# Delta-rule stage of a fp32 hybrid layer: base blocks and decay masks turned and filled on chip, low weight parts by accumulating transfers

## The chip, the cores and the metric

The kernel runs on one core of one Trainium2 chip. The metric is the device time of one execution in microseconds. A core has TensorE (PE, whose weight loads are listed apart as PEld), VectorE (DVE), ScalarE (ACT), GpSimd (POOL) and SyncE (SP). Here nearly all transfers are issued from SP's queue.

## The reference

One layer over 512 latent tokens of width 1024, with 256 context tokens: half-step SwiGLU FFN, then two mixers side by side (neighbourhood attention; bidirectional gated DeltaNet) merged by sigmoid gates, then a second half-step FFN. The change lies in the gated delta rule, which works on chunks of 64 tokens:

```python
    decay = jnp.exp(jnp.where(lower, g[..., :, None] - g[..., None, :], -jnp.inf))
    m = jnp.where(strict, jnp.einsum('...ik,...jk->...ij', k_beta, k) * decay, 0.0)
    rhs = jnp.concatenate([v * beta[..., None], k_beta * jnp.exp(g)[..., None]], axis=-1)
    uw = lax.linalg.triangular_solve(jnp.eye(GDN_CHUNK) + m, rhs, left_side=True, lower=True, unit_diagonal=True)
    def step(s, xc):
        v_new = xc[0] - jnp.einsum('...ck,...kv->...cv', xc[1], s)
        s_next = s * xc[3][..., None, None] + jnp.einsum('...ck,...cv->...kv', xc[2], v_new)
        return s_next, (jnp.einsum('...ck,...kv->...cv', xc[4], s) + jnp.einsum('...cj,...jv->...cv', xc[5], v_new))
```

There are four heads and two directions. The kernel takes chunks of 128 tokens, six in each direction (two of context, four of latent), and inverts the 128 x 128 triangular matrices explicitly.

## The kernel before

Matrix products in fp32 are made of three: a weight tile is split into a high part `wh` (a rounded copy, ACT, line 137) and a low part `wl` (weight minus high part, DVE, line 139), an activation likewise into `uxh` and `uxl`, and hi·hi, hi·lo and lo·hi are accumulated (`mm3k`, lines 192 to 194). Class `Stream` loads the next weight block (`wr`, 512 KB, SP) and splits it, one block ahead, into two buffers each of `wh` and `wl`.

Projections of the mixers whose results are needed only later (queries, keys and values of the attention, `qa`, `ka`, `va`, and the gates `ga`, `gb`) are "fills": each is 24 matmuls of 128x512 into one accumulator `pm`, copied out by ACT (`spill`) and stored to DRAM. They are cut into FS = 4 quarters of six matmuls. In the delta-rule stage, `turn(kind, i)` adds a rate from the table `RATE` (g: Grams, l: ahead of the first inversion, i: inversions, s: scan) to a running debt and emits a quarter for each whole unit, marked to be issued behind the last delta-rule matmul. So PE has fill work to do while the other engines finish what the next small delta-rule matmul needs. 24 fills stand in this stage. The text is given to a scheduler that orders each engine's instructions by a modelled timeline; `issue_after` marks add edges to it.

The delta rule itself goes by steps s = 0 to 5 (one chunk in each direction) and head pairs p = 0, 1; two steps make a batch, bi = 0, 1, 2. The stage's parts are:

- `gram(p, s)`: the row of cumulated decay logs `gcd` is loaded over all partitions into `Dt` (256 KB; for s below 3 into parts of `oacc`). DVE subtracts the column and adds the triangular mask, four times 128x128 (line 1122), ACT takes the exponential over 512 columns (line 1123). DVE multiplies product, beta and decay into `Bt` (line 1128), stored to DRAM as `bd`, and for s of 2 and over product and decay into `At` (line 1134). Products come from PE (`pq`) or, for s of 4 and 5, from copies in DRAM (`kq`).
- `base_inverse`, once a batch: 64 diagonal 32x32 blocks are inverted together, row by row. The blocks come back from `bd` by six kinds of loads with short pieces into `L` and `Ltr`; ACT turns `Ltr` (line 1153), POOL fills the diagonal (line 1155) and the start `Xt`. Then 31 rows follow, each a product and a reduction on DVE (lines 1159, 1160). `Xt` is stored to DRAM as `rd`.
- `inverse(bi, st)`, twice a batch: the inverted blocks are read from `rd` into `T0` and `T1` (SP, eight transfers a batch), DVE transposes the other halves (lines 1182, 1183), ACT and POOL copy them into `T6` and `Tt` (line 1194). Then the blocks grow 32 to 64 to 128 by PE products `pi`, with DVE copies `Y` (lines 1202, 1229) and negated results written into `T6` (DVE, line 1218) and `Tt` (ACT, lines 1219, 1237) between them.
- `scan_step(p, s)`: the recurrence on the states `S`, PE products `pc` with DVE and ACT work between them.
- `gdn_out`: norm and gate, then the stage is over.

The program's order is: Grams and base blocks of batch 0, Grams of batch 1, inversions of batch 0 with the rows of batch 1 between them, scans of batch 0 with the Grams of batch 2, and so on, so that the rows of one batch run beside the inversions and scans of the one before. POOL's queue before holds only memsets, the `Tt` copies and a few small operations in this stage.

Of the kernel before, what the change touches and what calls it, by code (L numbers as in the profile page):

```python
# [58 lines left out]
def body(ctx, tc, I, out, dbg=None):  # L59
# [96 lines left out]
    class Stream:  # L156

        def __init__(self, wp, srcs, bufs, ahead):  # L160
# [946 lines left out]
    def decay_place(s, p):  # L1107

        if s == 2 or s < 2 and p == 1:
            a = 2 * (s == 2)  # L1110
            return oaccs[p if s == 2 else s][:, a:a + 2].rearrange("p a b c -> p (a b) c")
        return tl(gb_, [P, 4, P], "Dt", 2)[:]

    def gram(p, s, bd, g):
# [3 lines left out]
        nc.sync.dma_start(Dt[:], bass.AP(gcd.tensor, gcd.offset + (4 * s + 2 * p) * P, [[0, P], [24 * P, 2], [1, 2 * P]]))  # L1118
        for m, (d, c, i) in enumerate(mats):
            msk = cst[:, (C_MF if d == 0 else C_MB):][:, 0:P]  # L1120
            with tc.issue_after(marks["At" if s > 3 else "Bt"]) if s > 1 else nullcontext():
                V.scalar_tensor_tensor(Dt[:, m], Dt[:, m], gcum[:, d, s, 2 * p + i:2 * p + i + 1], msk, op0=ALU.subtract, op1=ALU.add)
        S.activation(Dt[:], Dt[:], AF.Exp)
        Bt, At = tl(gq, [P, 4, P], "Bt", NBT), None
        for n, t in enumerate(products(p, s)):
            if n == 0:
                for m, (d, c, i) in enumerate(mats):
                    b = V.scalar_tensor_tensor(Bt[:, m], t[m] if s == 1 else t[:, m], beta[:, d, s, 2 * p + i:2 * p + i + 1], Dt[:, m], op0=ALU.mult, op1=ALU.mult)
# [11 lines left out]
    def base_inverse(bd, rd):  # L1140


        L = tl(gb_, [P, 32, 32], "L")
# [9 lines left out]
        S.copy(L[0:64].rearrange("p r c -> p c r"), tr[:])

        G.memset(L[:].rearrange("p r c -> p (r c)")[:, 0:1024:33], -1.0)
        for i in range(1, 32):
# [3 lines left out]
            V.tensor_reduce(Xt[:, 0:c, i], t[:, 0:c, 0:i + 1], AX, ALU.add, negate=True)  # L1160
# [12 lines left out]
    def inverse(bi, st, rd, Bts):  # L1173


        T0 = tl(gq, [P, 8, 32], "T0", 2)
        T1 = tl(gq, [P, 8, 32], "T1", 2)
        for dst, d in ((T1, 0), (T0, 1)):
            for q in range(2):
                nc.sync.dma_start(dst[q:P:2, 4 * d:4 * d + 4], bass.AP(rd.tensor, rd.offset + (2 * d + q) * 16384 + st * 2048, [[32, 64], [2 * 2048, 4], [1, 32]]))  # L1180
# [737 lines left out]
```

## Time and profile before

| what | value |
|---|---|
| median of 3 runs | 1499.81 us (1499.24 to 1501.12) |
| profiled execution | 1495.44 us |
| its span | 1493.7 us |
| mean granted PE clock | 0.993 |
| PE busy, whole span | 1434.0 us (96%) |
| DVE / ACT / POOL busy, whole span | 1144.7 / 661.9 / 212.4 us |
| delta-rule stage | 733.2 to 966.4 us of the span |

Busy times are of the profiled execution; the engine idle least, PE, is the one on which most of the chain of waits lies (71% of it), with transfers at 10% and DVE at 9%. Weight loads (PEld) overlap the matmuls. A wait line "PE pi L1049 <- DVE Y L1229" reads: a matmul of line 1049 into `pi` waited for DVE's write of `Y` on line 1229.

### The profile page before, as it was taken

Reading aid. Unit: us, or ns where it says so; the run is one execution under the profiler, and the core shown is the slowest. Engines: PE = TensorE matmul, PEld = TensorE weight load, DVE = VectorE, ACT = ScalarE, POOL = GpSimd, SP = SyncE. Lnnn points to the kernel's source line nnn. Section 1 sums busy time; section 2 is a strip of 40 time slices with the busy share of each in tenths; the row PEclk is TensorE's granted clock in tenths of the full one; section 3 lists DMA queues with packets and bytes.
Section 4 is the critical chain, followed back from the end, with each engine's and each line's share of the span. In section 5 each row is a group of like instructions: output and inputs, shape, how many; then the busy total and the mean of one; then the engine's idle time right before and its main releaser. Section 6 shows DMA issues by size and latency. Waiting matters only on the chain.

```text
span 1493.7 us, 23926 instructions
## 1 busy us (share of the span) xinstructions
PE 1434.0 (96%) x9117; PEld 1258.3 (84%) x9117; DVE 1144.7 (77%) x1975; ACT 661.9 (44%) x1090; POOL 212.4 (14%) x262
## 2 busy tenths in 40 slices
PE   6999999999999999999998899999999999999997
PEld 4778989999998777888886778877778999998886
DVE  8787869999987565768787886666668799886627
ACT  5433524434333286545544434376526454444310
POOL 1000000000000121223301002243321022220001
PEclk9999999999999999999999999999999999999999
DMA  9676665454559554222577524274344143234732
GB/s 372 211 257 225 222 238 187 137 174 166 170 198 404 181 178 129 84 92 88 159 222 203 167 68 125 92 276 131 100 169 149 64 129 113 85 114 134 263 98 84
DMA packets 109236, 248.56 MB, mean 166 GB/s; under 512 B 29049, under 2 KB 44481, under 8 KB 109121
## 3 DMA queue, kind: packets, MB, share of 16 engines
q1 hardware_dynamic: 104480, 229.40, 46.6%
q0 software_dynamic: 3056, 12.33, 2.2%
q10 hardware_dynamic: 1586, 5.32, 0.9%
q8 instruction: 71, 1.16, 0.3%
q14 instruction: 43, 0.35, 0.1%
HBM read 215.50 MB, written 31.50 MB: 165 GB/s over the span
## 4 chain that ended last, share of the span: by engine, by line
PE 71%; DMA 10%; DVE 9%; ACT 4%; issue 3%; POOL 1%; SPq 1%; DVEq 0%; ACTq 0%; POOLq 0%
PE ps L211 15%; PE pm L192 5%; PE pm L193 5%; PE pm L194 5%; PE ps L533 4%; PE ps L535 4%; PE ps L534 4%; PE ps L1692 3%; PE ps L1694 3%; PE ps L1693 3%; PE ps L193 3%; PE ps L192 3%; PE ps L194 3%; PE pc L1049 3%; DMA wr<-in_up_dram 2%
## 5 line engine op out<-in xcount | busy, mean ns | idle before, releaser
L139 DVE TENSOR_TENSOR wl<-wr,wh 128x1024 fp32r<-128x1024 f32 (+1 forms) x184 | 226.0, 1233 | 112.9 <-ACT wh L137 111.3
L137 ACT CAST wh<-wr 128x1024 fp32r<-128x1024 f32 (+1 forms) x184 | 185.6, 1013 | 278.5 <-PE pm L193 72.7
L192 PE MATMUL pm<-uxh,wh 128*128 128x512 f32 x320 | 131.6, 411 | 0.0
L194 PE MATMUL pm<-uxh,wl 128*128 128x512 f32 x320 | 126.3, 395 | 0.8 <-DVE wl L139 0.8
L193 PE MATMUL pm<-uxl,wh 128*128 128x512 f32 x320 | 126.5, 395 | 0.0
L211 PE MATMUL ps<-wh,hx 128*128 128x512 f32 x352 | 96.1, 391 | 0.1
L211 PEld LDWEIGHTS ps<-wh,hx 128*128 128x128 f32 x352 | 65.9, 188 | 14.5 <-ACT wh L137 0.5
L280 DVE SCALAR_TENSOR_TENSOR adap<-wr,crow 128x1024 f32<-128x1024 f32 x61 | 74.3, 1218 | 2.4 <-DMA wr<-in_w_adaT_dram 1.7
L192 PE MATMUL ps<-uh,wh 128*128 128x256 f32 (+1 forms) x208 | 69.2, 334 | 3.8 <-ACT wh L137 3.8
L194 PEld LDWEIGHTS pm<-uxh,wl 128*128 128x128 f32 x320 | 60.6, 190 | 13.8 <-DVE wl L139 0.9
L192 PEld LDWEIGHTS pm<-uxh,wh 128*128 128x128 f32 x320 | 60.8, 190 | 11.1 <-ACT spill L796 0.2
L193 PEld LDWEIGHTS pm<-uxl,wh 128*128 128x128 f32 x320 | 60.9, 190 | 10.3
L114 POOL TENSOR_TENSOR rs<-ve,mhalf 128x1 f32<-128x1 f32 (+2 forms) x46 | 49.0, 1066 | 140.6 <-DVE ve L110 138.2
L193 PE MATMUL ps<-ul,wh 128*128 128x256 f32 (+1 forms) x208 | 67.9, 327 | 0.0
L194 PE MATMUL ps<-uh,wl 128*128 128x256 f32 (+1 forms) x208 | 67.0, 328 | 0.0
L193 PE MATMUL ps<-uxl,wh 128*128 128x256 f32 (+1 forms) x192 | 60.5, 318 | 2.2 <-DVE uxl L139 2.2
L192 PE MATMUL ps<-uxh,wh 128*128 128x256 f32 (+1 forms) x192 | 59.8, 318 | 1.6 <-ACT uxh L137 1.4
L194 PE MATMUL ps<-uxh,wl 128*128 128x256 f32 (+1 forms) x192 | 60.1, 316 | 0.0
L137 ACT CAST wh<-ra 128x1024 fp32r<-128x1024 f32 x31 | 32.6, 1052 | 59.7 <-PE ps L534 20.2
L533 PE MATMUL ps<-ur,wh 128*128 128x384 f32 x168 | 56.5, 336 | 0.0
L534 PE MATMUL ps<-ur,wh 128*128 128x384 f32 x168 | 56.4, 336 | 0.0
L533 PE MATMUL ps<-uh,wh 128*128 128x384 f32 x168 | 56.4, 336 | 0.0
(502 smaller groups left out, 4252.0 us busy)
## 6 DMA issues: line engine op xcount, KB each, us to landing
wr<-in_w_adaT_dram SPq DMA_DIRECT2D x64, 512.0 KB, 4.7
wr<-in_up_dram SPq DMA_DIRECT2D x56, 512.0 KB, 3.6
wr<-in_win_dram SPq DMA_DIRECT2D x52, 512.0 KB, 3.6
wr<-in_dn_dram SPq DMA_DIRECT2D x51, 512.0 KB, 4.1
ra<-in_up_dram SPq DMA_DIRECT2D x24, 512.0 KB, 4.3
rb<-in_up_dram SPq DMA_DIRECT2D x18, 512.0 KB, 4.0
ra<-in_w_adaT_dram SPq DMA_DIRECT2D x16, 512.0 KB, 5.0
wr<-in_w_o_dram SPq DMA_DIRECT2D x8, 512.0 KB, 4.4
```

What stands on the lines that cost most here:

```text
L114: G.tensor_tensor(rs[:], ve[:], mhalf[:, 0:n], ALU.pow)
L137: S.copy(hi, src)
L139: marks["lo"] = V.tensor_tensor(lo, src, hi.bitcast(F32), ALU.subtract).ins
L192: T.matmul(ps, a, uh[:, k, :], start=(k == 0), stop=False)
L193: T.matmul(ps, a, ul[:, k, :], start=False, stop=False)
L194: marks["mm"] = T.matmul(ps, b, uh[:, k, :], start=False, stop=(k == nk - 1)).ins
L211: T.matmul(banks[t][d][:, c0:c1], a[:, sl], b[:, d * 512 + c0:d * 512 + c1], start=first and j == 0, stop=last and j == 2)
L280: V.scalar_tensor_tensor(pr[:], raw[:], 1.0, crow, op0=ALU.mult, op1=ALU.mult, accum_out=col[:, c:c + 1])
L533: T.matmul(ps[:], a, mh, start=k == 0, stop=False)
L534: T.matmul(ps[:], a, ml, start=False, stop=False)
L535: T.matmul(ps[:], b, mh, start=False, stop=k == 3)
L1049: last[0] = T.matmul(*a, **k).ins
```

## The change

Five things are changed together, all in the delta-rule stage.

1. **Low parts.** For the 24 fills of the stage (`ws.dma`), DVE's subtraction goes. ACT writes the negated high part into `wl`, in two halves, and POOL issues for each half a transfer of 256 KB from `wr` onto `wl` that adds to what is there. Every fill now does its 16 products with the high part first and its eight with the low part last (also where the low parts are made as before).
2. **Base blocks.** The way through DRAM (`bd`) goes. ACT copies the diagonal blocks from `Bt` into a tile `W` (four copies a Gram, 48 in all); DVE transposes part of `W` in 32x32 blocks, then all of it into `L`, and sets the diagonal. The start of `Xt` is loaded from a constant, `xt0`.
3. **Inverted rows.** The way through DRAM (`rd`) goes. DVE transposes `Xt` into `Z`, ACT copies halves into `T0` and `T1` (two copies for each of the two inversions), DVE transposes the other halves.
4. **Masks.** For s of 2 and over SP loads the mask (`msk`, a constant of 256 KB) into the decay tile and POOL issues a transfer that adds the row; ACT takes the exponential per matrix, 128x128, with the negated column as its bias. For s below 2 it stays as before. `issue_after` marks put the row for s = 5 behind the `Tt` copies and the exponentials behind the W copies of the batch before or, for s = 5, behind the last `Tt` write. For s = 3 the decay tile is now a buffer `r`.
5. **Rates.** g (2, 3.0, 0.7) to (2, 2.4, 0.6); l 7.2 to 2; i (1.5, 0, 0) to (1.2, 0.2, 0.7); s (0.7, 0.9, 0.5) to (0.6, 0.8, 0.9). The number of fills in the stage stays 24.

The core of the diff:

```diff
+    def split_dma(src, hi, lo):
+        S.copy(hi, src)
+        n = src.shape[-1] // 2
+        for h in (slice(0, n), slice(n, 2 * n)):
+            S.activation(lo[:, h], hi[:, h].bitcast(F32), AF.Copy, scale=-1.0)
+            G.dma_start(lo[:, h], src[:, h], accum_op=ALU.add)
...
-        for k in range(KT):
-            if k and k % (KT // parts) == 0:
+        prods = [(w[0], u, k) for k in range(KT) for u in (uxh, uxl)] + [(w[1], uxh, k) for k in range(KT)]
+        for n, (a, u, k) in enumerate(prods):
+            if n and n % (3 * KT // parts) == 0:
                 yield
-            mm3k(px[:], w[0], w[1], uxh, uxl, k)
+            marks["mm"] = T.matmul(px[:], a[:, k * P:k * P + P], u[:, k, :], start=n == 0, stop=n == 3 * KT - 1).ins
...
-    RATE = {"g": (2, 3.0, 0.7), "l": (7.2,), "i": (1.5, 0, 0), "s": (0.7, 0.9, 0.5)}
+    RATE = {"g": (2, 2.4, 0.6), "l": (2,), "i": (1.2, 0.2, 0.7), "s": (0.6, 0.8, 0.9)}
...
+    def blocks(W, Bt, p, st):
+        m0 = 4 * st + p
+        for b in range(4):
+            r = slice(32 * b, 32 * b + 32)
+            marks["W"] = S.copy(W[r, 8:24].rearrange("p (d m) c -> p d m c", d=2)[:, :, m0:m0 + 3:2], Bt[r, :, r].rearrange("p (d i) c -> p d i c", d=2)).ins
...
+        if s > 1:
+            nc.sync.dma_start(Dt[:], I["msk"])
+            with tc.issue_after(marks["Tt"]) if s > 4 else nullcontext():
+                G.dma_start(Dt[:], row, accum_op=ALU.add)
+        else:
+            nc.sync.dma_start(Dt[:], row)
...
+            if s > 1:
+                with tc.issue_after(marks["Ti" if s > 4 else "Wg"]):
+                    S.activation(Dt[:, m], Dt[:, m], AF.Exp, bias=ngc[:, d, s, 2 * p + i:2 * p + i + 1])
...
-                nc.sync.dma_start(bass.AP(bd.tensor, bd.offset + g * MSTR, [[P, P], [4 * MSTR, 4], [1, P]]), Bt[:])
+                blocks(W, Bt, p, s % 2)
...
-        for q in range(4):
-            dst = tr[32 * q:32 * q + 32] if q < 2 else L[32 * q:32 * q + 32]
-            nc.sync.dma_start(dst, bass.AP(bd.tensor, bd.offset + (q // 2) * 8 * MSTR, [[st, 32], [P, 32], [1, 32]]))
-        S.copy(L[0:64].rearrange("p r c -> p c r"), tr[:])
-        G.memset(L[:].rearrange("p r c -> p (r c)")[:, 0:1024:33], -1.0)
+        with tc.issue_after(marks["Z"]) if "Z" in marks else nullcontext():
+            V.transpose(W[:, 0:8].rearrange("p m c -> p (m c)"), W[:, 16:24].rearrange("p m c -> p (m c)"))
+        V.transpose(L[:].rearrange("p r c -> p (r c)"), W[:, 0:16].rearrange("p m c -> p c m")[:, :, None].to_broadcast([P, 32, 2, 16]))
+        V.memset(L[:].rearrange("p r c -> p (r c)")[:, 0:1024:33], -1.0)
...
-        nc.sync.dma_start(bass.AP(rd.tensor, rd.offset, [[512, P], [1, 512]]), Xt[:].rearrange("p c k -> p (c k)"))
+        Z = tl(gb_, [P, 16, 32], "bt")
+        marks["Z"] = V.transpose(Z[:].rearrange("p c k -> p (c k)"), Xt[:].rearrange("p c k -> p (c k)")).ins
+        z = Z[:].rearrange("p c (q m) -> p m (c q)", q=2)
+        for st in range(2):
+            S.copy(T0[:, 0:4], z[:, 4 * st + 8:4 * st + 12])
+            S.copy(T1[:, 4:8], z[:, 4 * st:4 * st + 4])
+            V.transpose(fl(T1, 0), fl(T0, 0))
+            V.transpose(fl(T0, 4), fl(T1, 4))
```

How the instructions stand is shown at three places. The first is PE ahead of the first inversion of batch 0; `pm` is the accumulator of a fill, `pi` of the inversion, `Bt` the product blocks. Before:

```order
L194 MATMUL pm_7609<-uxh_4690,wl_7572 128x512
L192 MATMUL pm_7609<-uxh_4690,wh_7571 128x512
L193 MATMUL pm_7609<-uxl_4691,wh_7571 128x512
L194 MATMUL pm_7609<-uxh_4690,wl_7572 128x512
L192 MATMUL pm_7609<-uxh_4690,wh_7571 128x512
L193 MATMUL pm_7609<-uxl_4691,wh_7571 128x512
L194 MATMUL pm_7609<-uxh_4690,wl_7572 128x512
L1049 MATMUL pi_7644<-T_1408_7628,Bt_7012 32x32 x4
L1049 MATMUL pi_7644<-T_1408_7628,Bt_7042 32x32 x4
L1049 MATMUL pi_7644<-T_1408_7628,Bt_7012 32x32 x4
L1049 MATMUL pi_7644<-T_1408_7628,Bt_7042 32x32 x4
```

and with the change:

```order
L803 MATMUL pm_7559<-uxl_4691,wh_7481 128x512
L803 MATMUL pm_7559<-uxh_4690,wl_7482 128x512 x8
L803 MATMUL pm_7596<-uxh_4690,wh_7552 128x512
L803 MATMUL pm_7596<-uxl_4691,wh_7552 128x512
L803 MATMUL pm_7596<-uxh_4690,wh_7552 128x512
L803 MATMUL pm_7596<-uxl_4691,wh_7552 128x512
L803 MATMUL pm_7596<-uxh_4690,wh_7552 128x512
L803 MATMUL pm_7596<-uxl_4691,wh_7552 128x512
L1064 MATMUL pi_7611<-T_1341_7253,Bt_7015 32x32 x4
L1064 MATMUL pi_7611<-T_1341_7253,Bt_7051 32x32 x4
L1064 MATMUL pi_7611<-T_1341_7253,Bt_7015 32x32 x4
L1064 MATMUL pi_7611<-T_1341_7253,Bt_7051 32x32 x4
```

Before, nine fills and three quarters of the tenth stand between the start of the stage and the first `pi`; now seven and a quarter, and the eight products with `wl` stand together at a fill's end.

The second is DVE at the last rows of batch 0's base blocks. Before, a low part and the decay of the next Gram follow, and `T0`, `T1` are turned among the rows of batch 1 (line 1182, not in this piece):

```order
L1159 TENSOR_TENSOR bt_7234<-L_7133,Xt_7135 128x15x31
L1160 TENSOR_REDUCE Xt_7135<-bt_7234 128x15
L1159 TENSOR_TENSOR bt_7237<-L_7133,Xt_7135 128x512
L1160 TENSOR_REDUCE Xt_7135<-bt_7237 128x16
L139 TENSOR_TENSOR wl_7572<-wr_7569,wh_7571 128x1024
L1122 SCALAR_TENSOR_TENSOR Dt_8159<-Dt_8159,gcum_5208,cst_5205 128x128 x4
L1159 TENSOR_TENSOR bt_7803<-L_7789,Xt_7791 128x2
L1160 TENSOR_REDUCE Xt_7791<-bt_7803 128x1
```

With the change, `Xt` is turned into `bt` (the tile of `Z`), `W` and `L` of batch 1 are made, and the four transposes of both inversions follow before the first row of batch 1; the low part and line 1122 are gone from here:

```order
L1184 TENSOR_TENSOR bt_7248<-L_7154,Xt_7006 128x512
L1185 TENSOR_REDUCE Xt_7006<-bt_7248 128x16
L1189 STREAM_TRANSPOSE bt_7251<-Xt_7006 128x512
L1178 STREAM_TRANSPOSE W_7265<-W_7265 128x256
L1179 STREAM_TRANSPOSE L_7743<-W_7265 128x1024
L1180 MEMSET L_7743 128x32
L1166 TENSOR_TENSOR At_7548<-pq_7540,r_7501 128x512
L1197 STREAM_TRANSPOSE T_1342_7254<-T_1341_7253 128x128
L1198 STREAM_TRANSPOSE T_1341_7253<-T_1342_7254 128x128
L1197 STREAM_TRANSPOSE T_1344_7260<-T_1343_7259 128x128
L1198 STREAM_TRANSPOSE T_1343_7259<-T_1344_7260 128x128
L1184 TENSOR_TENSOR bt_7747<-L_7743,Xt_7266 128x2
```

The third is POOL in the first part of the stage. Before it has memsets and `Tt` copies:

```order
L942 TENSOR_TENSOR ktok_5216<-t_1255_6810,t_1256_6811 128x512
L1170 MEMSET T_1275_6933 128x512
L1170 MEMSET Tt_1276_6934 128x1024
L1170 MEMSET Tt_1277_6935 128x1024
L1155 MEMSET L_7133 128x32
L1155 MEMSET L_7789 128x32
L1146 MEMSET Xt_8305 128x512
L1148 MEMSET Xt_8305 32x16 x4
L1194 COPY Tt_1276_6934<-T_1409_7629 32x8x32 x4
L1194 COPY Tt_1277_6935<-T_1447_7852 32x8x32 x4
L1155 MEMSET L_8303 128x32
L1194 COPY Tt_1276_6934<-T_1561_8417 32x8x32 x4
```

With the change, rows onto masks (line 1146, from `gcd`) and low parts (line 146, from `wr`) stand ahead of the `Tt` copies (line 1222) in one queue:

```order
L146 DMA wl_7083<-wr_7080 128x512 x2
L1146 DMA r_7424<-gcd_5197 128x2x256
L1146 DMA r_7501<-gcd_5197 128x2x256
L1146 DMA Dt_8060<-gcd_5197 128x2x256
L1146 DMA Dt_8093<-gcd_5197 128x2x256
L146 DMA wl_7120<-wr_7117 128x512 x2
L146 DMA wl_7294<-wr_7291 128x512 x2
L146 DMA wl_7364<-wr_7361 128x512 x2
L146 DMA wl_7411<-wr_7408 128x512 x2
L146 DMA wl_7482<-wr_7479 128x512 x2
L146 DMA wl_7553<-wr_7550 128x512 x2
L1222 COPY Tt_1277_6936<-T_1342_7254 32x8x32 x4
```

More of the change, by code (lines that the diff above doesn't have):

```diff
@@ L176, in fill @@
                 lo = tl(p, [P, D], "wl", bufs, F32R)
-                split(raw[:, 0:c], hi[:, 0:c], lo[:, 0:c], self.behind.get(self.i, ()))
+                if self.dma:
+                    split_dma(raw[:, 0:c], hi[:, 0:c], lo[:, 0:c])
+                else:
+                    split(raw[:, 0:c], hi[:, 0:c], lo[:, 0:c], self.behind.get(self.i, ()))
                 self.q.append((hi, lo))
@@ L1042, in body @@
     FS, N0, NKQ, NLATE = 4, 2, 2, 3
-    RATE = {"g": (2, 3.0, 0.7), "l": (7.2,), "i": (1.5, 0, 0), "s": (0.7, 0.9, 0.5)}
+    RATE = {"g": (2, 2.4, 0.6), "l": (2,), "i": (1.2, 0.2, 0.7), "s": (0.6, 0.8, 0.9)}
     NBT, NAT, NT6, NTT = 8, 8, 1, 2
+    ngc = tl(gq, [P, 2, 6, 4], "ngc")
+    S.activation(ngc[:], gcum[:], AF.Copy, scale=-1.0)
     last = [None]
@@ L1111, in decay_place, with gram @@
             return oaccs[p if s == 2 else s][:, a:a + 2].rearrange("p a b c -> p (a b) c")
+        if s == 3:
+            return tl(gq, [P, 4, P], "r", 2)[:]
         return tl(gb_, [P, 4, P], "Dt", 2)[:]
-    def gram(p, s, bd, g):
+    def blocks(W, Bt, p, st):
[3 more added lines that the diff above has]
+            marks["W"] = S.copy(W[r, 8:24].rearrange("p (d m) c -> p d m c", d=2)[:, :, m0:m0 + 3:2], Bt[r, :, r].rearrange("p (d i) c -> p d i c", d=2)).ins
+    def gram(p, s, W):
         mats = mats_of(s)
         Dt = decay_place(s, p)
-        nc.sync.dma_start(Dt[:], bass.AP(gcd.tensor, gcd.offset + (4 * s + 2 * p) * P, [[0, P], [24 * P, 2], [1, 2 * P]]))
-        for m, (d, c, i) in enumerate(mats):
-            msk = cst[:, (C_MF if d == 0 else C_MB):][:, 0:P]
-            with tc.issue_after(marks["At" if s > 3 else "Bt"]) if s > 1 else nullcontext():
+        row = bass.AP(gcd.tensor, gcd.offset + (4 * s + 2 * p) * P, [[0, P], [24 * P, 2], [1, 2 * P]])
+        if s > 1:
+            nc.sync.dma_start(Dt[:], I["msk"])
+            with tc.issue_after(marks["Tt"]) if s > 4 else nullcontext():
+                G.dma_start(Dt[:], row, accum_op=ALU.add)
+        else:
+            nc.sync.dma_start(Dt[:], row)
+        for m, (d, c, i) in enumerate(mats):
+            if s > 1:
+                with tc.issue_after(marks["Ti" if s > 4 else "Wg"]):
+                    S.activation(Dt[:, m], Dt[:, m], AF.Exp, bias=ngc[:, d, s, 2 * p + i:2 * p + i + 1])
+            else:
+                msk = cst[:, (C_MF if d == 0 else C_MB):][:, 0:P]
                 V.scalar_tensor_tensor(Dt[:, m], Dt[:, m], gcum[:, d, s, 2 * p + i:2 * p + i + 1], msk, op0=ALU.subtract, op1=ALU.add)
-        S.activation(Dt[:], Dt[:], AF.Exp)
+        if s < 2:
+            S.activation(Dt[:], Dt[:], AF.Exp)
         Bt, At = tl(gq, [P, 4, P], "Bt", NBT), None
@@ L1171, in body, with inverse @@
     inv_n = [0]
[L1173 to L1180, printed above, removed]
-        fl = lambda t, m: t[:, m:m + 4].rearrange("p m c -> p (m c)")
-        V.transpose(fl(T0, 0), fl(T1, 0))
-        V.transpose(fl(T1, 4), fl(T0, 4))
+    def inverse(bi, st, Bts):
+        T0, T1 = turned.pop(0)
         blk = [slice(32 * b, 32 * b + 32) for b in range(4)]
@@ L1338, in inv_of @@
     def inv_of(bi, st):
-        inv[(bi, 2 * st)], inv[(bi, 2 * st + 1)] = inverse(bi, st, rds[bi], [res[(bi, 2 * st + p)][0] for p in range(2)])
+        inv[(bi, 2 * st)], inv[(bi, 2 * st + 1)] = inverse(bi, st, [res[(bi, 2 * st + p)][0] for p in range(2)])
     def scan_of(bi, j):
@@ L1346, in body @@
         next(fills)
+    ws.dma = True
     step(grams(0))
@@ L1833, in _consts, with _start @@
     return c
+def _start():
+    t = np.zeros((P, 16, 32), np.float32)
+    for q in range(2):
+        for c in range(16):
+            t[np.arange(P) % 32 // 16 == q, c, 2 * c + q] = 1.0
+    return t.reshape(P, 512)
 def _rope():
@@ L1872, in layout @@
     a["cst"] = _consts()
+    a["xt0"] = _start()
+    a["msk"] = np.repeat(a["cst"][:, C_MF:C_MF + 2 * P].reshape(P, 2, 1, P), 2, 2).reshape(P, 4, P)
     a["rope"] = _rope()
```

38 lines of the change are left out of this document (19 added, 19 removed).

## The prediction

> **What bounds the kernel now.** I read the stage that the change touches first: the delta-rule stage, from the first Gram matmuls at 733.20 to 966.40 us of the span. The view by windows gives it in one row, then in three parts (start and first base block; batches 0 and 1; the rest). Columns: window, its length, busy us and count on PE, PEld, DVE, ACT and POOL, then the granted clock, the DMA share and GB/s.
>
> ```profile
> 733.20:966.40 233.20, 215.87 (x1845) 181.05 (x1844) 173.80 (x470) 93.32 (x182) 28.51 (x51) 0.99 0.50 153
> 733.20:802.00 68.80, 62.86 (x316) 52.69 (x315) 53.04 (x153) 28.53 (x39) 1.31 (x7) 1.00 0.80 235
> 802.00:867.00 65.00, 59.42 (x608) 47.81 (x608) 52.76 (x156) 28.49 (x61) 7.54 (x17) 0.97 0.55 161
> 867.00:966.40 99.40, 93.59 (x922) 80.54 (x923) 68.00 (x163) 36.30 (x82) 19.66 (x27) 0.98 0.28 90
> ```
>
> PE is busy 215.87 of 233.20 us. The change touches no matmul's shape or number here, so the 17.33 us in which PE idles (5.94, 5.58 and 5.81 by part) are all there is to win. PE's own waits say what ends that idle time (total us, times, longest):
>
> ```profile
> PE pi L1049 <- DVE Y L1229: 5.1, 3, 2.4
> PE pi L1049 <- DMA T<-rd: 4.3, 1, 4.3
> PE pc L1049 <- DVE bt L1159: 1.8, 1, 1.8
> PE pi L1049 <- DVE T L1218: 1.6, 2, 1.0
> PE pc L1049 <- ACT Tt L1237: 0.9, 2, 0.5
> PE pm L194 <- DVE wl L139: 0.8, 1, 0.8
> ```
>
> One is a transfer, the way of the base blocks through DRAM; most others are small DVE operations on the inversion's chain that come late because DVE is full of other work. PE's timeline shows the one wait, and the price of a fill beside it:
>
> ```profile
> 794.79 0.39 PE L192 MATMUL pm<-uxh,wh 128*128 128x512 f32 x1
> 797.28 0.39 PE L194 MATMUL pm<-uxh,wl 128*128 128x512 f32 x1
> 802.00 0.92 PE L1049 MATMUL pi<-T,Bt 32*32 32x32 f32 x32 [4.33 <-DMA T<-rd]
> ```
>
> Eleven starts lie between 794.79 and 797.28: 0.226 us a matmul, 5.43 us a fill of 24. The chain of waits gives the base block's way before that (start, us, what):
>
> ```profile
> 739.49 4.14 DVE Bt L1128 x16
> 745.13 4.14 DMA bd<-Bt
> 751.22 4.44 DMA L<-bd
> ...
> 790.12 0.70 DVE Xt L1160
> ...
> 816.63 6.17 DMA Dt<-gcd
> ```
>
> **The first inversion, the largest single wait.** DVE's timeline around it, and its hold between the first and the last row of the base block:
>
> ```profile
> 738.28 1.22 DVE L139 TENSOR_TENSOR wl<-wr,wh 128x1024 fp32r<-128x1024 f32 x1
> 755.99 0.16 DVE L1159 TENSOR_TENSOR bt<-L,Xt 128x2 f32<-128x2 f32 x1 [5.03 <-POOL L L1155]
> 755.99:790.82 34.83, 33.25 (x92) 1.00 0.75 230
> 755.99:790.82 34.83, 6.17 (x6) 1.00 0.75 230
> ```
>
> (The third row is DVE's busy time in that stretch, the fourth what line 139 has of it.) The last product block is ready at 743.6 and the rows start at 755.99: 12.4 us in DRAM. Without line 139 at 738.28 the blocks end near 742.4. Four ACT copies follow, and DVE transposes of 128x256 and 128x1024; before has only 128x128 ones. The rows that price all these parts:
>
> ```profile
> L1159 DVE TENSOR_TENSOR bt<-L,Xt 128x2 f32<-128x2 f32 (+30 forms) x93 | 32.2, 346 | 8.5 <-POOL L L1155 6.4
> L1160 DVE TENSOR_REDUCE Xt<-bt 128x1 f32<-128x2 f32 (+30 forms) x93 | 31.6, 339 | 2.2
> L139 DVE TENSOR_TENSOR wl<-wr,wh 128x1024 fp32r<-128x1024 f32 (+1 forms) x26 | 31.2, 1201 | 2.9 <-PE pi L1049 1.5 <-ACT wh L137 1.4
> L1122 DVE SCALAR_TENSOR_TENSOR Dt<-Dt,gcum,cst 128x128 f32<-128x128 f32 x24 | 6.8, 346 | 7.8 <-DMA Dt<-gcd 7.8
> L1182 DVE STREAM_TRANSPOSE T<-T 128x128 f32<-128x128 f32 x6 | 1.8, 303 | 3.5 <-DMA T<-rd 3.5
> L137 ACT CAST wh<-wr 128x1024 fp32r<-128x1024 f32 (+1 forms) x26 | 26.7, 1028 | 68.2 <-PE pm L193 55.2 <-issue 11.8 <-DMA wr<-in_win_dram 1.2
> L798 ACT ACTIVATE spill<-pm 128x512 f32<-128x512 f32 x16 | 9.4, 589 | 0.0
> L1219 ACT ACTIVATE Tt<-pi 32x128 f32<-32x128 f32 x24 | 6.4, 268 | 4.8 <-PE pi L1049 4.5
> L1093 ACT COPY kq<-pq 128x512 f32<-128x512 f32 x8 | 4.6, 581 | 9.5 <-PE pq L1049 4.1 <-issue 2.3 <-ACT spill L798 2.0
> L1153 ACT COPY L<-Ltr 64x1024 f32<-64x1024 f32 x3 | 6.3, 2111 | 3.3 <-DMA Ltr<-bd 3.3
> L1123 ACT ACTIVATE Dt<-Dt 128x512 f32<-128x512 f32 x6 | 3.8, 632 | 16.0 <-DVE Dt L1122 16.0
> L1274 ACT ACTIVATE ktail<-ktok,etg 128x128 f32<-128x128 f32 x36 | 11.5, 390 | 11.5 <-PE pc L1049 11.5
> L561 POOL DMA_DIRECT2D hd<-ur x7 | 3.8, 540 | 98.8 <-DVE ur L560 98.8
> ```
>
> W copies 4 x 0.268 = 1.1 us. A transpose of 1024 elements a partition lies between one operation of that width (1.20) and eight of 128 elements (8 x 0.303 = 2.42), one of 256 between 0.30 and 0.61; I take 2.4 for both, nearer the row that is a transpose, and 0.3 for the memset. The rows then start near 742.4 + 1.1 + 2.4 + 0.3 = 746.2, some 9.8 us sooner. The rest of DVE's stretch shrinks by line 139 (6.2) and four of line 1122 (4 x 0.346 = 1.4): 34.8 - 7.6 = 27.2, to about 773.5. Z (1.2), the second batch's W, L and memset (2.7), one 692 ns At, four ACT copies of which two overlap, and two pairs of transposes (4 x 0.3) bring T0 and T1 to about 780. PE would have reached the first inversion matmul at 797.7 (797.28 + 0.39); the order puts 7.25 fills ahead of it instead of 9.75, so 2.5 x 5.43 = 13.6 us are kept for later, and PE comes at about 783 once the 1.6 us of other idle there (5.94 - 4.33) are gone. Ready at 780, wanted at 783: the 4.3 us wait falls away with up to 3 us to spare, and the fills kept back cover batches 0 and 1, where PE now waits on DVE.
>
> **DVE, over the stage.** 24 of line 139 go, 24 x 1.201 = 28.8 us, and 32 of line 1122's 40 (24 on Dt above, 16 on oacc), 32 x 0.346 = 11.1. Added are three W and L transposes with memset (3 x 2.7), three Z (3 x 0.7 to 1.2), and the T transposes stay in number: 10 to 12 us. DVE falls from 173.8 to about 145. Off the path this is nothing; on it, it shortens the queue ahead of Y and T (5.1 + 1.6 us of PE waits) and bt and wl (1.8 + 0.8).
>
> **ACT, the price.** Negated high parts 48 x 0.589 = 28.3 (the 128x512 spill is the nearest row); W copies 48 x 0.268 = 12.9; T copies 12 x 0.390 = 4.7; exponentials 32 x 0.390 for 8 x 0.632, +7.4; line 1153 gone, -6.3. ACT goes from 93.3 to about 140 of 233 us. Between the first W copies and the T copies, 740 to 780, its order has 28 W copies (7.5), 24 exponentials (9.4), 7 high parts (7.2), 7 spills (4.1), 14 negations (8.3), 8 kq copies (4.6) and 4 T copies (1.6): 42.7 us in 40. There it has no slack; the T copies stand last in that queue and may come near 783 instead of 780, just when PE wants them. Behind them wait T0, T1 and every inversion matmul.
>
> **POOL and the low parts.** 48 + 8 transfers x 0.540 us to issue = 30 us on a POOL that is busy 28.5 of 233. What counts is L, the time from issue to landing. No transfer of before accumulates; POOL's own are the nearest of its kind (KB each, median us to landing; then minimum, median and maximum of the last), and SP's of 256 KB in this stage the nearest in size:
>
> ```profile
> hd<-ur POOLq DMA_DIRECT2D x7, 384.0 KB, 2.8
> xr<-x1d POOLq DMA_DIRECT2D x4, 512.0 KB, 6.5
> DMA to landing us min/median/max: 4.0/6.5/9.9
> bd<-Bt SPq DMA_DIRECT2D x12, 256.0 KB, 5.2
> ```
>
> Two buffers hold the weights, so a low part may be written once the last matmul of the fill before last is over, and the new product order needs it 16 matmuls into the next but one: 5.43 + 16 x 0.226 = 9.05 us later in dense fills. (The high part's buffer is free 8 matmuls earlier, so its copy is over by then.) In that time ACT does the spill and two negations and POOL issues: 0.59 + 2 x 0.59 + 0.54 = 2.31. The low part is hidden up to L = 9.05 - 2.31 = 6.74, and each us beyond costs PE one for each dense fill. Bounds of L: 2.8 below, 9.9 above. I take 5 to 6, the row of the same size, though from another queue. Dense are about nine fills (7.25 ahead of the first inversion and a few late): up to 6.74 they cost nothing, at 9.9 they cost 9 x 3.16 = 28 us. Elsewhere scan work stands between the quarters of a fill, its period is about 233.2 / 24 = 9.7 us, and the margin 4.3 us larger: even 9.9 is hidden.
>
> [...]
>
> **Masks, start and transfers.** 51 loads and stores go (12 bd, 12 into L and Ltr, 3 rd, 24 T), many in small pieces while DMA is at 0.80 of its time; 11 come (8 msk, 3 xt0) and 8 rows move to POOL. I count this as nothing, since it hides beside fills; without that cover it is a gain. A row must now land after its mask, two transfers in turn where one took 6.17 us in the chain at 816.63. There is most of a batch for it, but it stands on POOL's queue ahead of low parts and Tt copies that wait behind it. For that and for ACT's fullness I put 2 us on the path (bounds 0, and 6.2 for one transfer laid bare).
>
> **The sum.** Won back by part: 5 of 5.94 (the 4.33 and most of the rest), 3.5 of 5.58, 1.5 of 5.81 (its waits are scan chains that stay). 10 less 2 is 8 us. The profiled execution took 1495.44 us with a span of 1493.7; 1487.4 there. The median of the runs is 1499.81, so 1491.8.
>
> **Rivals.** *Everything is won* (0.20): DVE at 145 leaves no queue, the waits on Y, T and bt go too, -16: 1484. For it: nearly every wait names DVE or the DRAM way. Against: an inversion is a serial chain whose DVE steps have nothing queued ahead in some places.
>
> *The wait only changes its name* (0.15): ACT, full in the first part, delivers the W and T copies late by what the DRAM way cost PE (4.3), and the inversion's own waits on Y and T stay (5.1 + 1.6) since they follow matmuls, not a queue: of the 10 won, 9 are lost, about 1499. For it: 42.7 us in 40. Against: ACT's excess is 2.7 us, while the DRAM way took 12.4 us ahead of the rows and 11 behind them (790.82 to 802.00).
>
> *Low parts land late* (0.18), the case on the other side. It costs 9 x (L - 6.74), decides from L = 7.6, where that is 8 us, and at the upper bound of 9.9 gives 1491.8 + 28 = 1520. For it: no row shows an accumulate, which also has to read where it writes, and xr reached 9.9. Against: its source lies on chip, it has half of xr's bytes, and bd, like it in size, took 5.2 with DMA at 0.80.
>
> [...]
>
> **How the numbers follow.** The forecast (-8) has 0.47, and alone a range of 1487 to 1497. Full gain reaches down to 1482, late low parts up to 1520; with the outer part of these two left out, 1482 to 1508 holds 8 in 10. 0.2% (3 us) is about what a measurement of this kernel can tell from no change. Faster, below 1496.8: 0.20, 0.43 of the 0.47 and 0.02 of the renamed wait, 0.65. Slower, above 1502.8: 0.16 of the late case and 0.02 of the renamed wait, 0.18. The same: 0.17.
>
> **What would show it.** Right: no PE wait on T before the first pi; the first base row near 746; DVE near 145 and ACT near 140 us in the stage; the wl transfers landing within 6.7 us; PE idle near 9 us. Wrong: waits of the 17th matmul of fills on the wl transfer (the late case), PE or DVE waits on ACT's W copies (the renamed one), L over 7.6 us, or DVE transposes well over 2.4 us, which would move the first inversion past 783.

## The result and the profile after

The changed kernel takes 1515.57 us (median of 4, 1514.82 to 1516.42) against 1499.53 before: ratio 1.0106, interval 1.0088 to 1.0123. It is 16 us slower, where 8 us less was forecast. The profiled executions have spans of 1513.0 and 1493.7 us. The latter was a fast one: 1495.44 us where the runs have 1499.5.

The stage now lies between 736.38 and 980.28 us. The view by windows, in the same three parts (columns as in the prediction):

```profile
736.38:980.28 243.90, 222.29 (x1844) 183.35 (x1843) 149.23 (x425) 136.02 (x310) 76.32 (x99) 0.96 0.72 180
736.38:798.71 62.33, 53.46 (x256) 43.14 (x254) 40.09 (x116) 40.98 (x98) 19.93 (x21) 0.95 0.90 219
798.71:870.00 71.29, 59.09 (x651) 47.36 (x652) 53.44 (x174) 43.66 (x107) 20.95 (x32) 0.90 0.77 193
870.00:980.28 110.28, 109.74 (x940) 92.85 (x939) 55.70 (x137) 51.38 (x106) 35.45 (x47) 1.00 0.58 150
```

The stage is 10.7 us longer (243.9 for 233.2). DVE and ACT are as busy as forecast (149 and 136 us, for 145 and 140). PE idles 21.6 us (17.3 before), and the granted clock is 0.96 where it was 0.99. So only 4.3 of the 10.7 us are more idle time; the other 6.4 are PE's busy time, 222.3 us for 215.9 with the same number of matmuls. Of the rest of the spans' difference, 3.2 us lie ahead of the stage and 5.4 behind it. PE's largest waits from 733 to 1000 us (the third lies behind the stage), and the last one on T:

```profile
PE pm L803 <- DMA wl<-wr: 8.3, 6, 3.2
PE pi L1064 <- DVE Y L1257: 7.5, 2, 6.4
PE pt L1461 <- ACT pT L1495: 4.9, 1, 4.9
PE pc L1064 <- DVE r L1288: 4.8, 3, 4.0
PE pi L1064 <- DVE T L1198: 0.6, 1, 0.6
```

The wait for T from DRAM is gone, but low parts (8.3) and an inversion's Y (6.4 at once) have come in. Rows picked from DVE's timeline at the first base block:

```profile
748.27 0.45 DVE L1178 STREAM_TRANSPOSE W<-W 128x256 f32<-128x256 f32 x1 [2.84 <-ACT W L1136]
748.75 1.91 DVE L1179 STREAM_TRANSPOSE L<-W 128x1024 f32<-128x1024 f32 x1
750.75 0.09 DVE L1180 MEMSET L<- 128x32 f32 x1
750.87 0.16 DVE L1184 TENSOR_TENSOR bt<-L,Xt 128x2 f32<-128x2 f32 x1
764.34 0.69 DVE L1166 TENSOR_TENSOR At<-pq,oacc 128x512 f32<-128x512 f32 x1 [3.72 <-ACT kq L1108]
771.02 0.61 DVE L1162 SCALAR_TENSOR_TENSOR Bt<-pq,beta,oacc 128x128 f32<-128x128 f32 x2 [3.34 <-ACT kq L1108]
792.18 0.71 DVE L1189 STREAM_TRANSPOSE bt<-Xt 128x512 f32<-128x512 f32 x1
797.55 0.69 DVE L1166 TENSOR_TENSOR At<-pq,r 128x512 f32<-128x512 f32 x1 [1.82 <-ACT kq L1108]
798.80 0.31 DVE L1198 STREAM_TRANSPOSE T<-T 128x128 f32<-128x128 f32 x1
809.52 0.69 DVE L1166 TENSOR_TENSOR At<-kq,Dt 128x512 f32<-128x512 f32 x1 [6.21 <-DMA kq<-kqd]
812.81 0.42 DVE L1257 COPY Y<-pi 128x256 f32<-128x256 f32 x1
```

The rows start at 750.87 and end at 792.15: 41.3 us, where before had 34.8 and the prediction 27.2. The window and DVE's waits in it say why:

```profile
750.87:792.15 41.28, 26.94 (x81) 0.92 0.90 214
```

```profile
DVE At L1166 <- ACT kq L1108: 8.7, 4, 3.7
DVE Bt L1162 <- ACT kq L1108: 5.7, 2, 3.3
```

(The first is DVE alone in that window; the waits are of 750.87 to 799.) DVE works 26.9 us there, near the 27.2 forecast for the whole stretch, and stands still for the rest. Products of batch 1's Grams stand between the rows in its queue, and they wait for ACT's copies. So T is finished at 799, not at 780. PE comes to it at 798.1, not at 783: all 8.3 us of waits on low parts lie ahead of this inversion, and its 256 matmuls up to there take 53.5 us, where 62.86 less 13.6 for the fills kept back would be 49.3 (the granted clock is 0.95). The timeline's last two rows show the next stall: an `At` waits 6.2 us for `kq` from DRAM, the copy Y stands behind it on DVE, and PE waits 6.4 us for Y.

ACT and SP show what holds them. ACT's group of high parts (busy and mean ns, then idle before it), SP's longest waits in the stage, and, in the last row, the longest of the run with the blocks alone (below):

```profile
L142 ACT CAST wh<-wr 128x1024 fp32r<-128x1024 f32 x24 | 25.1, 1047 | 37.5 <-PE pm L803 21.3 <-DMA wr<-in_win_dram 15.9
```

```profile
SPq L183 <- DMA wl<-wr: 128.0, 26, 10.9
```

```profile
SPq L815 <- ACT spill L811: 53.0, 11, 14.9
```

The adding transfer reads the raw weight `wr`. Until it has landed, that buffer cannot take the next weight: SP's loads wait 128 us for it in all, and ACT waits 15.9 us for late weights (1.2 before), with kq copies and T copies behind in its queue (one such wait of 2.74 us ends at 759.94, and the next kq copy starts at 763.65). The sum of SP's waits says little by itself: in the run with the blocks alone SP waits 121 us for three kinds of spill. At the stage's start POOL's rows come on top:

```profile
741.63 2.57 POOL L1146 DMA_DIRECT2D oacc<-gcd  x2 [9.49 <-DMA oacc<-in_msk_dram]
743.22 2.80 POOL L146 DMA_DIRECT2D wl<-wr  x2
744.34 4.16 POOL L1146 DMA_DIRECT2D r<-gcd  x2
745.86 5.12 POOL L1146 DMA_DIRECT2D Dt<-gcd  x2
```

Six rows and the first low part were issued within 10 us, and PE waited 3.2 us for that low part, at 751.5.

### The profile page after: what moved, and what is told of

Read it like the earlier page. It is cut to its first block, busy times and chain, and to the rows that moved or that the text cites. A ratio compares the mean times of both kernels' runs of the same rounds, so it can differ in the third digit from the quotient of the medians.

```text
span 1513.0 us, 24000 instructions
## 1 busy us (share of the span) xinstructions
PE 1445.7 (96%) x9117; PEld 1265.2 (84%) x9117; DVE 1120.6 (74%) x1931; ACT 705.4 (47%) x1220; POOL 256.9 (17%) x300
## 4 chain that ended last, share of the span: by engine, by line
PE 70%; DMA 11%; DVE 9%; issue 4%; ACT 4%; POOL 2%; SPq 1%; DVEq 0%; ACTq 0%; POOLq 0%
PE ps L223 15%; PE pm L803 6%; PE ps L547 4%; PE ps L545 4%; PE ps L546 4%; PE pc L1064 3%; PE ps L1724 3%; PE ps L1726 3%; PE ps L1725 3%; PE pm L204 3%; PE pm L206 3%; PE pm L205 3%; PE ps L204 3%; PE ps L205 3%; PE ps L206 3%
## 5 line engine op out<-in xcount | busy, mean ns | idle before, releaser
L138 DVE TENSOR_TENSOR wl<-wr,wh 128x1024 fp32r<-128x1024 f32 (+1 forms) x160 | 196.6, 1235 | 113.3 <-ACT wh L136 108.1
L136 ACT CAST wh<-wr 128x1024 fp32r<-128x1024 f32 (+1 forms) x160 | 160.5, 1008 | 214.0 <-PE ps L223 42.8
L803 PE MATMUL pm<-uxh,wh 128*128 128x512 f32 x224 | 93.4, 417 | 0.0
L803 PE MATMUL pm<-uxl,wh 128*128 128x512 f32 x224 | 89.0, 397 | 0.0
L803 PE MATMUL pm<-uxh,wl 128*128 128x512 f32 x224 | 65.3, 421 | 8.3 <-DMA wl<-wr 8.3
L146 POOL DMA_DIRECT2D wl<-wr x48 | 43.9, 1074 | 131.7 <-ACT wl L145 105.2
L546 PE MATMUL ps<-ul,wh 128*128 128x384 f32 x168 | 56.4, 336 | 0.0
L547 PE MATMUL ps<-ur,wl 128*128 128x384 f32 x168 | 56.3, 335 | 0.0
L547 PE MATMUL ps<-uh,wl 128*128 128x384 f32 x168 | 56.3, 336 | 0.0
L223 PE MATMUL ps<-wl,hh 128*128 128x512 f32 x176 | 55.3, 389 | 0.0
```

The costliest lines, as they stand in the source:

```text
L136: S.copy(hi, src)
L138: marks["lo"] = V.tensor_tensor(lo, src, hi.bitcast(F32), ALU.subtract).ins
L223: T.matmul(banks[t][d][:, c0:c1], a[:, sl], b[:, d * 512 + c0:d * 512 + c1], start=first and j == 0, stop=last and j == 2)
L546: T.matmul(ps[:], a, ml, start=False, stop=False)
L547: T.matmul(ps[:], b, mh, start=False, stop=k == 3)
L803: marks["mm"] = T.matmul(px[:], a[:, k * P:k * P + P], u[:, k, :], start=n == 0, stop=n == 3 * KT - 1).ins
```

## The experiments

Each was compared with the kernel before on the same chip; "us" are of ratio times 1500. The parts taken one by one came first.

**Low parts back on DVE, all else changed.**

```diff
-    ws.dma = True
+    ws.dma = False
```

> The changed kernel (1515.6) with one part undone: the low parts of the stage's weights come from DVE's subtraction again, not from negations on ACT and adding transfers of POOL. Theory A (the low parts' new way is the cause: the transfer's source is the raw weight itself, so its buffer is held until the sum has landed, the next weight loads late, ACT waits for it with all that stands behind): 1492 to 1501, that is 15 us or more come back, and the wait of the inversion on Y (6.4 us) is gone. Rival B (the rows added onto masks, six of them at once at the stage's start, fill POOL's queue and the transfers): under 5 us come back, 1511 or more. Rival C (the rates, which keep 2.5 fills back from the first inversion): under 5 us come back.

Measured: 1510.03 us, ratio 1.0057 (1.0039 to 1.0076). 7 us come back of 16, where theory A asked for 15 and its rivals for under 5: theory A explains half at most, and something else costs 8.5 us. Its profile has a wait ahead of the first inversion that is 0.6 us in the changed kernel's:

```profile
797.52 0.65 PE L1064 MATMUL pi<-T,Bt 32*32 32x32 f32 x32 [5.88 <-DVE T L1198]
```

**The low parts alone, with their product order, on the kernel before.**

```diff
+    def split_dma(src, hi, lo): ...
...
+    ws.dma = True
     step(grams(0))
```

> The kernel before (1499.5) with only the new low parts and the product order that goes with them; blocks, masks and rates as before. Theory A: slower than before by 8 to 16 us, 1507 to 1515, with ACT waiting on weight loads for 10 us or more in the stage (1.2 before). Rivals B and C: within 4 us of before.

Measured: 1518.72 us, 1.0113 (1.009 to 1.0136). ACT's waits on weight loads are 31.7 us. It is 17 us slower, just above theory A's range.

**A third raw buffer.**

```diff
-        t = tl(p, [P, NX], "spill", 2)
+        t = tl(p, [P, NX], "spill", 1 if p is spool1[0] else 2)
...
-        Y = tl(gq, [P, 4, 32], "Y2", 2)
+        Y = tl(gq, [P, 4, 32], "Y2", 1)
...
+        return tl(gb_, [P, D], "wr3") if nraw[0] % 3 == 0 else tl(wp, [P, D], "wr", WB)
...
+    ws.raw = raw3
```

> The changed kernel with a third buffer for the raw weights from the stage's start up to the attention's first loads (room made by one instead of two buffers of the fills' output and of Y). Theory A in its form 'the raw buffer is held too long': 6 to 12 us come back (1504 to 1510), and ACT's wait on weight loads in the first part falls from about 13 us to under 5. If the landing of the sums itself is what is late, or by rivals B and C: within 3 us of the changed kernel.

Measured: 1509.45 us, 1.0061 (1.0038 to 1.0084). ACT's waits on loads in the first part go from 9.5 us to none, and 7 us come back, which fits the held buffer. A later run below, with the same edit on another version, does not bear it out.

**Masks as before, all else changed.**

```diff
-            nc.sync.dma_start(Dt[:], I["msk"])
...
-                G.dma_start(Dt[:], row, accum_op=ALU.add)
...
+        nc.sync.dma_start(Dt[:], row)
...
```

> The changed kernel with the decay made as before (row loaded by SP, column and mask on DVE, one exponential of 512); low parts, blocks and rates as changed. Rival B: 8 us or more come back, 1507 or less. Theory A and rival C: under 4 us come back.

Measured: 1510.92 us, 1.006 (1.004 to 1.008): 7 us come back, between the ranges of theory A and rival B. PE's waits on low parts fall from 8.3 to 2.2 us, and one on T of 11 us appears. So the masks delay the low parts; whether through POOL's queue, which both share, or through ACT's exponentials, this run does not show.

None of the four is as fast as before. Theory D was formed from the waits on T: the rates, which keep fills back from the first inversion, take its cover away.

**Blocks alone** (old rates, old masks, low parts on DVE; the product order stays new).

> Of the change only the turned blocks and rows are left, with the product order of the fills; low parts on DVE, masks and rates as before. Theory D (the new rates take cover away, the blocks on chip are a gain by themselves): 1490 to 1498, faster than before (1501.5 in the last comparison), with no wait on T ahead of the first inversion. If the blocks on chip bring nothing or cost: 1500 or more.

Measured: 1487.97 us, 0.9918 (0.9901 to 0.9934): 12 us faster than before; no version of the study is better. Its stage, the one row of its PE timeline up to the first inversion with a wait of 0.2 us or more, and DVE's busy time from the first to the last row of the base block:

```profile
735.64:960.58 224.94, 215.38 (x1846) 180.50 (x1844) 183.63 (x482) 106.50 (x238) 27.04 (x43) 0.98 0.40 130
```

```profile
799.24 0.45 PE L1064 MATMUL pi<-T,Bt 32*32 32x32 f32 x32 [1.35 <-DVE T L1191]
```

```profile
755.91:791.73 35.82, 33.79 (x91) 1.00 0.56 184
```

T comes at 799 here too, with PE's fills reaching to 798: the wait is 1.35 us.

**The rates alone, on the kernel before.**

```diff
-    RATE = {"g": (2, 3.0, 0.7), "l": (7.2,), "i": (1.5, 0, 0), "s": (0.7, 0.9, 0.5)}
+    RATE = {"g": (2, 2.4, 0.6), "l": (2,), "i": (1.2, 0.2, 0.7), "s": (0.6, 0.8, 0.9)}
```

> The kernel before with the new rates alone: the base block's way goes through DRAM as before, so T is ready near 802 us, and PE has up to 2.5 fills (13.6 us) less to do until then. Theory D: slower by 8 to 14 us, 1509 to 1516, with a wait of 10 us or more on T. If the rates don't matter: within 3 us of before.

Measured: 1525.7 us, 1.0172 (1.0151 to 1.0192). 26 us slower, twice the expectation; the row is

```profile
805.02 0.65 PE L1049 MATMUL pi<-T,Bt 32*32 32x32 f32 x32 [16.36 <-DMA T<-rd]
```

**The changed kernel with the old rates** (the same two lines, the other way round).

> The changed kernel with the old rates: low parts, masks and blocks as changed. Theory D as the main cause: 1502 to 1508. Theory A as the main cause (low parts late, and more dense fills now ahead of the first inversion): 1512 or more, with PE's waits on low parts of 10 us or more (8.3 in the changed kernel).

Measured: 1517.61 us, 1.0112 (1.0094 to 1.0129). No gain. PE has no wait on T, but still 8.2 us of waits on low parts (10 or more were expected) and 4.6 us on a Y. Theory A fits here; the two costs do not add.

**Blocks and new rates.**

> Turned blocks, product order and the new rates; low parts on DVE and masks as before. It stands one step from two others. Against the run with the old rates in their place, theory D: slower by 5 to 10 us; without it, the same. Against the run that has the new masks too (1510.0, 8.5 above before): rival B (the rows added onto masks cost by themselves) says 5 us or more faster; without it, the same within 2.

Measured: 1509.92 us, 1.0066 (1.005 to 1.0082): 22 us slower than with the old rates, and no different from the run with the masks too. The stage has the same 1844 weight loads and is 16.7 us longer, with one wait of 12.0 us:

```profile
735.75:977.42 241.67, 217.26 (x1845) 180.94 (x1844) 183.29 (x481) 106.43 (x238) 24.12 (x43) 0.96 0.37 121
```

```profile
797.67 0.65 PE L1064 MATMUL pi<-T,Bt 32*32 32x32 f32 x32 [12.02 <-DVE T L1191]
```

**Blocks and masks, old rates.**

> Turned blocks and the new masks, old rates, low parts on DVE: one step from the run with the blocks alone (1488.0, ratio 0.9918). Rival B (rows added onto masks cost by themselves): 5 us or more above it. Otherwise, as the two runs with the new rates say (8.5 and 10.1 us above before): within 3 us of it, 1485 to 1491.

Measured: 1489.62 us, 0.9919 (0.9902 to 0.9937). Without the new low parts the masks cost nothing and bring nothing.

**Blocks and low parts, old rates and masks.**

> Turned blocks and the new low parts (negation on ACT, adding transfer on POOL), old rates and masks: one step from the blocks alone (1488.0). Theory A: the low parts cost 10 to 25 us, 1498 to 1513; what is left to the run with the masks as well (17.8 above before) is the part of the rows in POOL's queue. If the low parts only cost together with the rows: within 4 us of 1488.

Measured: 1506.34 us, 1.0029 (1.0012 to 1.0045): the low parts cost 16.6 us here. To the changed kernel with the old rates (1.0112) only the masks are missing: beside the new low parts they cost 12.4 us, where without them they cost nothing. PE's largest waits here:

```profile
PE pi L1064 <- DVE Y L1223: 5.1, 1, 5.1
PE pi L1064 <- DVE T L1239: 3.9, 1, 3.9
PE pm L803 <- DMA wl<-wr: 2.8, 4, 1.6
```

**ACT's added work alone.** The transfer is replaced by DVE's subtraction over ACT's negation:

```diff
-            G.dma_start(lo[:, h], src[:, h], accum_op=ALU.add)
+        V.tensor_tensor(lo, src, hi.bitcast(F32), ALU.subtract)
```

> Turned blocks, old rates and masks; ACT writes the two negated halves as in the change, and then DVE writes the difference over them: ACT's added work (some 28 us) alone, without a transfer, and with DVE's work as before. If ACT's fullness is what the new low parts cost: 10 us or more above the blocks alone, 1498 or more. Theory A, where the raw buffer is held by the transfer: within 4 us, 1484 to 1492.

Measured: 1490.26 us, 0.9923 (0.9898 to 0.9948). ACT's 28 us more (27.5 us in 48 negations) are free.

**The transfer alone.** The kernel leaves out the negation and the addition, so its low parts are the weights themselves:

```diff
-            S.activation(lo[:, h], hi[:, h].bitcast(F32), AF.Copy, scale=-1.0)
-            G.dma_start(lo[:, h], src[:, h], accum_op=ALU.add)
+            G.dma_start(lo[:, h], src[:, h].bitcast(F32R))
```

> Turned blocks, old rates and masks; the low part is only transferred from the raw weight by POOL, without a negation before and without an addition (the subtraction is left out, so the low parts are the weights themselves): the transfer and the held buffer alone, without ACT's added work and without DVE's. Theory A: most of the cost of the run with both, 8 us or more above the blocks alone. If ACT's fullness or the addition is the cause: within 4 us of 1488 or faster, as DVE is 29 us freer.

Measured: 1491.5 us, 0.9933 (0.991 to 0.9956). Free too, within the noise, against theory A; and DVE's 29 us less bring nothing. The views of the POOL queue's transfers and issues show what differs. First the run with negation and addition, then this one (queue: packets, MB, share of the 16 engines in 735 to 975; landing in us; POOL's group):

```profile
q0 software_dynamic: 6912, 12.59, 30.1%
wl<-wr POOLq DMA_DIRECT2D x48, 256.0 KB, 4.8
```

```profile
L146 POOL DMA_DIRECT2D wl<-wr x48 | 42.5, 1040 | 143.6 <-ACT wl L145 119.8 <-DMA r<-gcd 9.5 <-ACT T L1189 8.5
```

```profile
q0 software_dynamic: 6912, 12.59, 16.5%
```

```profile
DMA to landing us min/median/max: 2.2/3.2/8.0
```

```profile
L145 POOL DMA_DIRECT2D wl<-wr x46 | 24.4, 533 | 129.5 <-PE pm L802 108.3 <-PE pc L1063 8.4 <-DMA wr<-in_win_dram 6.4
```

For the same bytes the run with the addition has 1.8 times the share of the DMA engines, twice the issue and 1.6 us more to land.

**Negation, then a plain transfer** (the addition is left out).

```diff
-            G.dma_start(lo[:, h], src[:, h], accum_op=ALU.add)
+            G.dma_start(lo[:, h], src[:, h].bitcast(F32R))
```

> As the run with blocks and the new low parts (1.0029 of before; blocks alone 0.9918), but the transfer overwrites the negated half instead of adding to it (so the low part is the weight itself; the subtraction is left out). The chain is the same: high part, negation, issue, landing. If the chain through ACT and POOL that holds the raw buffer is what costs: 8 us or more above the blocks alone still. If the addition's own slowness is (issue 1.04 us against 0.53, landing 4.8 against 3.1, twice the share of the DMA engines for the same bytes): within 4 us of the blocks alone.

Measured: 1495.82 us, 0.9974 (0.9957 to 0.999). Half way: some 8 us of the 16.6 are the serial chain, the other half goes with the addition. Share (16.5%) and issue (0.54 us) are those of the transfer alone, and the median landing is 3.7 us, so 1.1 us of the 4.8 go with the addition.

**A third raw buffer on blocks and low parts.**

> As the run with blocks and the new low parts (1.0029), with a third buffer for the raw weights up to the attention's first loads (room by one buffer instead of two for the fills' output and for Y). If the held raw buffer is what costs: 8 us or more come back, 0.998 of before or less, and ACT's waits on weight loads fall from 33 us to under 15. If the addition's slowness or the deadline of the low part itself does: 4 us or less come back.

Measured: 1504.86 us, 1.0037 (1.0019 to 1.0054). ACT's waits on loads fall from 33 to 10.7 us, and the time stays. PE now waits 5.6 and 3.0 us for Y and 3.9 on low parts. The first of these stood there before (5.1), behind an `At` that waits for `kq` from DRAM (5.75 us without the third buffer, 7.08 with it). ACT's waits for a held buffer can thus fall without a gain. The test is not pure, since one of the two buffers of Y and of the fills' output went to make room.

**Blocks with the old product order.**

> Turned blocks alone, now also with the old order of a fill's products. The order moves the need for a low part later in the fill; with low parts from DVE early enough it should do nothing: within 3 us of the run with the new order (0.9918). If the order is itself part of the gain: 5 us or more slower; if part of the loss: faster.

**The new order alone, on the kernel before.**

> The kernel before with the new order of a fill's products alone. With blocks on chip the new order was worth 10 us (0.9918 against 0.9985). If it is a gain by itself: 0.995 or less. If it only pays together with the blocks (through the order the scheduler then makes): within 3 us of before.

Measured: 1497.26 us, 0.9985 (0.9968 to 1.0002), and 1498.92 us, 0.9992 (0.997 to 1.0015). Neither the blocks nor the order moves the time by itself; together they gain 12 us. In the profiles the stage of the blocks with the old order is as short as with the new one (736.78 to 960.28 us, 223.5 for 224.9), and what it loses comes behind the stage (534 us to the end for 527). Of these 7 us, 5.0 are PE's busy time for the same 3432 matmuls (511.9 for 506.9 us): the granted clock is 0.89 for 1.00 in the first 30 us behind the stage. Why it falls there is open.

**Weights loaded from POOL's queue** (with blocks and low parts).

> As the run with blocks and the new low parts (1.0029 of before), with the stage's raw weights loaded from POOL's queue instead of SP's, so that a load that waits for its buffer no longer holds up SP's other transfers (spills, kq to DRAM and back, decay rows). If SP's blocked queue is what costs (SP waits 42 us on the adding transfers between 735 and 830, At on DVE then 5.8 us on kq, and Y behind At): 8 us or more come back, 0.997 or less, with At's wait on kq under 3 us. If the cost is in the chain hi, negation, addition, next load itself: within 4 us of 1.0029.

Measured: 1510.62 us, 1.0076 (1.0051 to 1.01). Slower, not faster: Y's long wait is gone (0.48 us for 5.1), and PE waits 5.9 us on low parts, 2.5 on a spill and 2.1 on another Y. The stall has moved.

**One rate alone** (l from 7.2 to 2, with blocks).

> The run with the blocks alone (0.9918), with one rate changed: l from 7.2 to 2, so that two quarters of a fill instead of seven stand between the last Gram product of batch 1 and the first inversion. If this cover is what the new rates take away: slower by 5 to 10 us than 0.9918, with a wait of 5 us or more on T. If the rates of Grams, inversions and scan are what cost: within 3 us.

Measured: 1502.4 us, 1.0022 (1.0005 to 1.004): 15.6 of the 22 us, more than expected, with the wait:

```profile
799.13 0.65 PE L1064 MATMUL pi<-T,Bt 32*32 32x32 f32 x32 [6.88 <-DVE T L1191]
```

## Why the prediction was wrong

Added up along one path, the difference is: blocks with the new order -12.3 us (0.9918), masks +0.2 (0.9919), rates +20.7 (1.0057), low parts +7.3 (1.0106), in sum +15.9. The order of the steps matters: with the old rates the low parts and masks together cost 29 us (0.9918 to 1.0112), and then the new rates win 1 us, which is within the noise.

- **The step that failed first is "T0 and T1 at about 780".** Most of its prices held: W and L turned in 0.45 and 1.91 us, memset 0.09 (2.4 and 0.3 assumed), rows at 750.9 (746.2 forecast, 3.2 of the difference being the stage's later start), DVE's work in the stretch 26.9 us (27.2). But I took DVE's work for the stretch's length. With low parts on ACT, the stretch is paced by products that wait for copies in ACT's queue (14.4 us of waits up to T). With them on DVE and the old rates and masks it is DVE's 33.8 us of work in 35.8 (32.1 in 38.5 with the new ones). In every version with the blocks on chip whose first inversion is shown above, T comes between 797 and 799.
- **So the fills kept back were no gift.** "PE at 783, ready at 780" was the place where 2.5 fills were booked as neutral. With low parts on DVE, PE came at 786 (797.67 less 12.02), about as forecast, and waited for T. In the changed kernel late low parts and the lower clock held PE back to 798.1. Along this path the term was the largest: +20.7 us. The rival that the wait changes its name was near (it saw ACT's full queue), but put it at nothing lost.
- **"Hidden up to L = 6.74" held for the median L and failed for its chain.** The transfer landed in 5.3 us (median; 3.2 to 10.0), as taken, and still PE waited 8.3 us on low parts. POOL's issue was put at 0.54 us and took 1.07 on average, 43.9 us for the 48. Left out of the 2.31 us were the load that waits for the raw buffer, ACT's queue standing behind it (15.9 us of ACT's waits), and POOL's rows. The late case of the rivals gave the right sign through another cause: it asked for L of 7.6.
- **The 2 us on the path for POOL and ACT** were too much for the masks alone (0.2) and much too little for low parts (7.3 to 17) and for both together (29 with the old rates).
- **"DVE shortens the queue ahead of Y and T"**: with 29 us less on DVE (the plain transfer) the time was that of the blocks alone. As far as that run shows, DVE's load was not what bounded the stage once the blocks stayed on chip, though DVE fell to 149 us nearly as forecast.
- **The blocks**: forecast as most of 10 us won, measured 12.3, but only together with the new product order.
- **Idle PE time was counted at its own length.** It can cost more, as the last section shows: in the stage 4.3 us more of it came with 6.4 us more of busy time.

Shown is that the new rates cost 21 to 26 us where low parts are on time (the l rate alone 16), by taking cover from the wait for T, and that the masks cost nothing alone and 7 to 12 us beside the new low parts. For the low parts it is shown that neither ACT's added work nor the transfer costs alone, that their chain costs 8 us and the addition as much again. By which queue the chain reaches PE was not settled: of three tries to free the raw buffer or its loads, one won 7 us, and two moved the stall and won nothing. How the masks slow the low parts is open too.

## What to carry over

An engine's busy time is not the length of its stretch when its queue holds work that waits for others (DVE's 26.9 us of work took 41.3 here): before moving cover away from a wait, look at the last thing in order ahead of what is awaited. Cover that is tuned to one version's finish should be moved only after that finish has been measured. And steps that are free one by one (a negation, a transfer, an added mask: 0.9923, 0.9933 and 0.9919 where the blocks alone have 0.9918) can cost much in one chain (1.0112 for all of them together, with the addition), so they should be measured together as well as apart.
